# A two-layer transformer kernel, down products of layer 0's experts: a third chunk buffer, loads asked for three chunks ahead, and the gate product placed just ahead of its reader

## The chip, the core and the metric

The kernel runs on one core of a Trainium2 chip as one program of 66,430 instructions. The core has four engines that compute: TensorE (PE, with its weight loads shown as PEld), VectorE (DVE), ScalarE (ACT) and GpSimd (POOL). Sixteen DMA engines move data between HBM and SBUF; transfers are asked for from queues, here that of SyncE (SP) for nearly all loads, that of ScalarE for writes, and that of GpSimd for gathers. Each engine and each queue works through its own list in order and waits on semaphores for the others. The metric is the device time of one execution in microseconds, as the median over runs.

## The reference

Two blocks of two layers each work on 256 tokens (and, in the first block, on 256 context tokens) of width 1024, in float32. The part that matters here is the expert stage of layer 0 of the first block, `peer_ffn`: each token picks, in 8 heads, 16 of 16,384 experts, whose up rows give a hidden value and whose down rows are summed up with gate times hidden value.

```python
def chunk(xc):
    ...
    top_s, pos = lax.top_k(cand, PEER_TOPK)
    eidx = jnp.take_along_axis(cidx, pos, axis=-1)
    gate = jax.nn.softmax(top_s, axis=-1)
    u = u_emb[eidx]
    hid = jax.nn.gelu(jnp.einsum('td,thkd->thk', xc, u))
    wgt = (gate * hid.astype(jnp.float32)).astype(xc.dtype)
    return jnp.einsum('thk,thkd->td', wgt, v_emb[eidx])
```

## The kernel before

For 384 of the 512 tokens of layer 0 the kernel does not gather expert rows. It computes the hidden values of all 16,384 experts (the up products, 128 steps of 128 experts, `"u"`), multiplies them by a dense matrix that holds the gates and zeros elsewhere, and multiplies the result with all down rows (the down products, 128 steps, `"vv"`). The last 128 tokens are gathered instead: `gathered()` fetches one row a token with an indirect DMA on GpSimd's queue (line 1399, four tiles `gr` in turn) and VectorE works on each (line 1408 for up rows, line 1423 for down rows). `sp` in the code is true in layer 0 alone.

Every float32 matrix product runs as three products of halves: ScalarE copies the high half (`wh`, `Wh`), VectorE subtracts it for the low half (`wl`, `Wl`). For streamed weights, `Stream` does this: `_load` asks for a 512 KB tile `raw` on SP's queue (line 200, five buffers), `_high` (line 212) and `_low` (line 223) split it two steps ahead of its use. The order of all streamed tiles is one list; down tiles (`in_vv`) and tiles for the next layer's modulation (`in_modt`, used by VectorE at line 516) alternate in it.

The up products write their hidden values through the tiles `gstage` (two steps of experts and 384 KB each, line 1642) to HBM, `gel` (line 1647), and the gate matrix is built beside them and written as `gmat` (line 1536). The down products read both back in 32 chunks of four steps:

- `wload(c)` (lines 1593 to 1598) asks on SP's queue for `gelc` and `gmc`, 768 KB each, two buffers each.
- `wmul(c)` (line 1604 in layer 0) multiplies `gelc` by `gmc` in place, on VectorE.
- `wsplit(i)` (line 1616, recorded at lines 472 and 473) splits the 384 columns of step i into `Wh` and `Wl`, four buffers each. It runs two steps ahead of the matmuls.
- `vmm` (line 1692) does 18 matmuls a step: three token tiles, three products of halves, two halves of the 1024 columns.

In step i, with chunk c and r = i mod 4, the calls stand in this order:

```python
if r == 0 and c + 1 < nch:
    wmul(c + 1)
if i + 2 < 128:
    wsplit(i + 2)
if r == CI - 1 and c + 2 < nch:
    wload(c + 2)
hl = W.next("vv", l, i, 1 if i >= 126 else None)
```

`W.next` is where the loads and the splits of later down tiles are put into the queues. The steps of `gathered()` are put between them by a planner, `Side`, which holds a clock of assumed costs: `tick` advances it with each group of matmuls, `took` charges VectorE or ScalarE. So a call that stands elsewhere also moves some gather steps on VectorE by a place or two. The first two chunks are asked for in step 118 of the up products, and `wmul(0)` runs in its step 125.

Of the kernel before, what the change touches and what calls it, by code (L numbers as in the profile page):

```python
# [10 lines left out]
F32 = mybir.dt.float32  # L11
F32R = mybir.dt.float32r
# [47 lines left out]
def late_v(i):  # L60

    n = (i - 1) * 48 // 122
    return (n,) if 0 < i <= 122 and n < i * 48 // 122 else ()
# [341 lines left out]
def tile_dit_peer_conformer(ctx: ExitStack, tc: tile.TileContext, A, out):  # L405
# [7 lines left out]
    def bankA():  # L413
        return psum.tile([128, 512], F32, name="pA", bufs=4)
# [51 lines left out]
    def mm3(o, s, m, start, stop):  # L466
        nc.tensor.matmul(o, s[0], m[0], start=start, stop=False)  # L467
        nc.tensor.matmul(o, s[0], m[1], start=False, stop=False)  # L468
        nc.tensor.matmul(o, s[1], m[0], start=False, stop=stop)  # L469

    def split(h, lo, src):
        nc.scalar.activation(h, src, AF.Copy)  # L472
        nc.vector.tensor_sub(lo, src, h.bitcast(F32))  # L473
# [37 lines left out]
    def mod_tile(l, n, S, junk):  # L511

        raw = W.next("modt", l, n)
        for s in range(2 if l == 0 or n < 16 else 1):
            o = modc[l][:, n, s:s + 1]
            nc.vector.scalar_tensor_tensor(junk, raw, 1.0, S[:, s], op0=OP.mult, op1=OP.mult, accum_out=o)
            spend("v", 1300)
        made.add((l, n))
        n0 = n // 8 * 8
        if all((l, n0 + k) in made for k in range(8)):  # L520
            g = modc[l][:, n0:n0 + 8, :]
            nc.vector.tensor_add(g, g, pc(l, "bmod")[:, n0:n0 + 8, None].to_broadcast([128, 8, 2]))
# [7 lines left out]
    def gate_row(pool, l, m, s):  # L530
        t = pool.tile([128, D], F32, name="grow", bufs=2)
        for hf in range(2):
            p = bankB()
            for j in range(4):
                nc.tensor.transpose(p[:, j * 128:(j + 1) * 128],
                                    modc[l][:, m * 8 + hf * 4 + j, s:s + 1].to_broadcast([128, 128]), ident)
            nc.scalar.activation(t[:, hf * 512:(hf + 1) * 512], p, AF.Copy)
        return t
# [110 lines left out]
    def tick(dt):  # L649
        if cur["side"] is not None:  # L650
            cur["side"].tick(dt)
# [618 lines left out]
    def peer(l, hcp, kp, keys, early):  # L1270
        last = l == NL - 1
        sp = not last
# [3 lines left out]
        TD = T - 128 if sp else T  # L1276
        ntd = TD // 128
        TB = 32
        ntb = TD // TB
        CI = 2048 // T  # L1280
# [4 lines left out]
        with ExitStack() as st:  # L1285
# [7 lines left out]
            gp = st.enter_context(tc.tile_pool(name=f"gel{l}", bufs=3))  # L1293
# [29 lines left out]
            def took(eng, ns):  # L1323
                return cur["side"].spend(eng, ns) if sp and cur["side"] else 0.0
# [265 lines left out]
            nch = 128 // CI  # L1590
            ld, ww = {}, {}

            def wload(c):
                g = vq.tile([128, CI, TD], F32, name="gelc", bufs=2)
                nc.sync.dma_start(g, gel_d[c])
                m = vq.tile([128, ntb, CI, TB], F32, name="gmc", bufs=2)
                nc.sync.dma_start(m, g_d[:, :, c * CI:(c + 1) * CI, :].rearrange("b p c t -> p b c t"))
                ld[c] = (g, m)

            def wmul(c):  # L1600
                g, m = ld[c]
                if sp:
                    gv = g.rearrange("p c (b t) -> p c b t", t=TB)
                    nc.vector.tensor_mul(gv, gv, m.rearrange("p b c t -> p c b t"))
                    took("v", 1770)
                    return
                for ci in range(CI):
                    gv = g[:, ci].rearrange("p (b t) -> p b t", t=TB)
                    nc.gpsimd.tensor_mul(gv, gv, m[:, :, ci])  # L1609

            def wsplit(i):
                c, r = divmod(i, CI)
                g = ld[c][0]
                wh = vp.tile([128, TD], F32R, name="Wh", bufs=4)
                wl = vp.tile([128, TD], F32R, name="Wl", bufs=4)
                split(wh, wl, g[:, r])
                if sp:
                    took("a", 470)
                    took("v", 560)
                ww[i] = (wh, wl)  # L1620

            gs = None
            b = None
            GB = 2 if not last else 4
            per = 512 // T
            for i in range(128):
                if i == WS:
                    wsplit(0)
                    wsplit(1)
                if i % GB == 0:  # L1630
                    gs = gp.tile([128, GB, TD], F32, name="gstage", bufs=3)
                h, lo = W.next("u", l, i)
                half = i % per
                if half == 0:
                    b = bankA()
                o = b[:, half * TD:(half + 1) * TD]
                for d in range(8):
                    mm3(o, (h[:, d * 128:(d + 1) * 128], lo[:, d * 128:(d + 1) * 128]), (X[0][:, d, :TD], X[1][:, d, :TD]), d == 0, d == 7)
                    tick(3 * TD / 2.4)
                if half == per - 1:  # L1640
                    j = i % GB - (per - 1)
                    nc.scalar.activation(gs[:, j:j + per].rearrange("p a t -> p (a t)"), b[:, :per * TD], AF.Gelu_apprx_tanh)
                    if sp:
                        took("a", 500)
                if i % GB == GB - 1:
                    c, r = divmod(i - GB + 1, CI)
                    nc.scalar.dma_start(gel_d[c][:, r:r + GB], gs)
                    if sp:
                        took("a", 340)
                if l == 0 and i in LATE:  # L1650
                    mod_tile(0, 40 + LATE.index(i), S, junk)
                if i == 118:
                    if sp:
                        side.finish(sel)
                    else:
                        side.drain()
                        cur["side"] = W.side = None
                    tk_stack.close()
                    vp = st.enter_context(tc.tile_pool(name=f"pv{l}", bufs=2))
                    vq_stack = ExitStack()  # L1660
                    vq = vq_stack.enter_context(tc.tile_pool(name=f"pw{l}", bufs=2))
                    wload(0)
                    wload(1)
                    if l == 0:
                        def turn():
                            for _ in angles(vq):
                                yield (side.spend("p", 2500.0) + 4000.0, None, 0, 0.0, 0.0, 0.0)
                        side.add(turn())
                        side.lanes.reverse()
                if i == 122:  # L1670
                    rows = [gate_row(vp, l, 5, s) for s in range(ns)]
                if i == 125:
                    wmul(0)
# [14 lines left out]
            def vmm(t, i, w, hl, halves=(0, 1)):  # L1688
                sh, sl = (x[:, t * 128:(t + 1) * 128] for x in w)
                for n, (s_, m_) in enumerate(((sh, hl[0]), (sh, hl[1]), (sl, hl[0]))):  # L1690
                    for dh in halves:
                        nc.tensor.matmul(acc[t][dh], s_, m_[:, dh * 512:(dh + 1) * 512],  # L1692
                                         start=(i == 0 and n == 0), stop=(i == 127 and n == 2))
                if sp:
                    tick(3 * len(halves) * 512 / 2.4)

            for i in range(128):
                c, r = divmod(i, CI)
                if r == 0 and c + 1 < nch:
                    wmul(c + 1)  # L1700
                if i + 2 < 128:
                    wsplit(i + 2)
                if r == CI - 1 and c + 2 < nch:
                    wload(c + 2)
                hl = W.next("vv", l, i, 1 if i >= 126 else None)
                if i >= 126:
                    held.append((i, ww.pop(i), hl))
                    continue
                w = ww.pop(i)
                for t in range(ntd):  # L1710
                    vmm(t, i, w, hl)
                for n in late_v(i) if sp else ():
                    mod_tile(l + 1, n, S, junk)
# [555 lines left out]
    with tc.tile_pool(name="hcp", bufs=1) as hcp:  # L2269
        tail = peer(0, hcp, kp, *first)  # L2270
        kp = ExitStack()
        first = mixer(1, kp, tail, done=xp)
    peer(1, None, kp, *first)
    with tc.tile_pool(name="b2", bufs=1) as b2p:
        dec = b2p.tile([128, RET_H, 384], F32, name="dec")
# [161 lines left out]
```

## Time and profile before

| | |
|---|---|
| median of 3 runs | 4544.48 us (4543.31 to 4550.07) |
| profiled execution, its own time | 4539.79 us |
| its span, first to last instruction | 4538.0 us |
| mean granted TensorE clock | 0.96 of full |
| PE / PEld busy | 4215.3 us (93%) / 3735.4 us (82%) |
| DVE busy | 3221.3 us (71%) |
| ACT busy | 1970.2 us (43%) |
| POOL busy | 1128.6 us (25%) |
| DMA | 932.29 MB, mean 205 GB/s |

The shares are means over stages with different limits. The down products of layer 0 lie between 1441 and 2213 us of the span. Engine names in the views are those given above; L1604 is line 1604 of the kernel; a group of instructions is named by its output and inputs, as `gelc<-gelc,gmc`; "idle before" is the time that the engine stood still just ahead of them, with the instruction or transfer that ended it. A DMA share is the busy share of the 16 DMA engines; packets of several queues can overlap, so it can pass 1.

### The profile page before, as it was taken

Reading aid. Unit: us, or ns where it says so; the run is one execution under the profiler, and the core shown is the slowest. Engines: PE = TensorE matmul, PEld = TensorE weight load, DVE = VectorE, ACT = ScalarE, POOL = GpSimd, SP = SyncE. Lnnn points to the kernel's source line nnn. Section 1 sums busy time; section 2 is a strip of 40 time slices with the busy share of each in tenths; the row PEclk is TensorE's granted clock in tenths of the full one; section 3 lists DMA queues with packets and bytes.
Section 4 is the critical chain, followed back from the end, with each engine's and each line's share of the span. In section 5 each row is a group of like instructions: output and inputs, shape, how many; then the busy total and the mean of one; then the engine's idle time right before and its main releaser. Section 6 shows DMA issues by size and latency. Waiting matters only on the chain. (4 is left out here: it accounts for less than half of the span.)

```text
span 4538.0 us, 66430 instructions
## 1 busy us (share of the span) xinstructions
PE 4215.3 (93%) x25423; PEld 3735.4 (82%) x25423; DVE 3221.3 (71%) x5177; ACT 1970.2 (43%) x2939; POOL 1128.6 (25%) x871
## 2 busy tenths in 40 slices
PE   8999999999998877777779989999999999999999
PEld 5887878999997666666678879999887998999988
DVE  6747766999996766566786878786666577555855
ACT  4224443334662222222334444575445445444544
POOL 0012343333117412222543446201443000000000
PEclk9999999999999888888899989999999999999999
DMA  6532232456889877878783336778886644556344
GB/s 218 166 99 69 72 101 97 151 194 234 293 293 343 278 259 270 289 276 283 249 301 110 107 124 206 237 282 306 281 280 237 215 154 132 187 181 215 116 160 156
DMA packets 304824, 932.29 MB, mean 205 GB/s; under 512 B 27752, under 2 KB 95736, under 8 KB 299640
## 3 DMA queue, kind: packets, MB, share of 16 engines
q1 hardware_dynamic: 244000, 696.86, 46.1%
q0 software_dynamic: 37040, 135.29, 8.3%
q10 hardware_dynamic: 23464, 95.88, 5.6%
q8 instruction: 199, 3.26, 0.3%
q14 instruction: 121, 0.99, 0.1%
HBM read 841.94 MB, written 85.99 MB: 204 GB/s over the span
## 5 line engine op out<-in xcount | busy, mean ns | idle before, releaser
L212 ACT ACTIVATE wh<-raw 128x1024 fp32r<-128x1024 f32 (+1 forms) x1086 | 1131.4, 1045 | 1093.4 <-DMA raw<-in_vv 516.4
L469 PE MATMUL pA<-xH,wl 128*128 128x256 f32 (+2 forms) x4600 | 1422.0, 309 | 57.3 <-DVE wl L223 46.1
L223 DVE TENSOR_TENSOR wl<-raw,wh 128x1024 fp32r<-128x1024 f32 (+2 forms) x956 | 1185.5, 1249 | 365.2 <-issue 185.5
L467 PE MATMUL pA<-xH,wh 128*128 128x256 f32 (+2 forms) x4600 | 1439.6, 313 | 1.7 <-ACT xH L472 1.3
L468 PE MATMUL pA<-xL,wh 128*128 128x256 f32 (+2 forms) x4600 | 1417.2, 308 | 0.5 <-DVE xL L473 0.3
L469 PEld LDWEIGHTS pA<-xH,wl 128*128 128x128 f32 x4600 | 876.1, 190 | 93.0 <-DVE wl L223 55.4
L467 PEld LDWEIGHTS pA<-xH,wh 128*128 128x128 f32 x4600 | 877.0, 191 | 34.8 <-issue 6.0
L468 PEld LDWEIGHTS pA<-xL,wh 128*128 128x128 f32 x4600 | 877.1, 191 | 26.6 <-DVE xL L473 1.1
L223 POOL TENSOR_TENSOR wl<-raw,wh 128x1024 fp32r<-128x1024 f32 (+1 forms) x130 | 322.8, 2484 | 731.8 <-PE pA L469 362.8
L1692 PE MATMUL pA<-wl,Wh 128*128 128x512 f32 x1024 | 349.9, 424 | 150.4 <-DVE wl L223 150.4
L1692 PEld LDWEIGHTS pA<-wl,Wh 128*128 128x128 f32 x1024 | 203.2, 202 | 211.1 <-DVE wl L223 163.9
L1692 PE MATMUL pA<-wh,Wl 128*128 128x512 f32 x1024 | 344.5, 419 | 1.7 <-DVE Wl L473 1.7
L1692 PE MATMUL pA<-wh,Wh 128*128 128x512 f32 x1024 | 335.3, 409 | 6.2 <-ACT Wh L472 6.2
L1399 POOL DMA_INDIRECT gr<-in_ur,gi x128 | 185.8, 1451 | 530.9 <-DVE gr L1408 498.8
L468 PE MATMUL pA<-wl,xH 128*128 128x256 f32 (+2 forms) x800 | 272.1, 340 | 10.2 <-POOL wl L223 6.2
L467 PE MATMUL pA<-wh,xH 128*128 128x256 f32 (+2 forms) x800 | 277.9, 347 | 1.8 <-ACT xH L472 1.8
L469 PE MATMUL pA<-wh,xL 128*128 128x256 f32 (+2 forms) x800 | 271.5, 339 | 1.1 <-DVE xL L473 1.1
L1399 POOL DMA_INDIRECT gr<-in_vr,gi x128 | 176.3, 1377 | 340.1 <-DVE gx L1423 297.7
L1609 POOL TENSOR_TENSOR gelc<-gelc,gmc 128x256 f32<-128x256 f32 x128 | 147.9, 1189 | 422.4 <-DMA gmc<-gmat 398.6
L1692 PEld LDWEIGHTS pA<-wh,Wl 128*128 128x128 f32 x1024 | 206.8, 202 | 54.5 <-DVE Wl L473 2.4
L1692 PEld LDWEIGHTS pA<-wh,Wh 128*128 128x128 f32 x1024 | 200.3, 196 | 56.2 <-ACT Wh L472 6.5
L458 POOL TENSOR_TENSOR segr<-segr,nhalf 128x1 f32<-128x1 f32 (+1 forms) x24 | 13.9, 579 | 886.3 <-DVE segr L547 886.3
(456 smaller groups left out, 6305.4 us busy)
## 6 DMA issues: line engine op xcount, KB each, us to landing
raw<-in_u SPq DMA_DIRECT2D x256, 512.0 KB
raw<-in_vv SPq DMA_DIRECT2D x256, 512.0 KB
raw<-in_modt SPq DMA_DIRECT2D x80, 512.0 KB
gmat<-gst ACTq DMA_DIRECT2D x20, 2048.0 KB
raw<-in_conv SPq DMA_DIRECT2D x48, 512.0 KB
raw<-in_gate SPq DMA_DIRECT2D x48, 512.0 KB
gel<-gstage ACTq DMA_DIRECT2D x64, 384.0 KB
gelc<-gel SPq DMA_DIRECT2D x32, 768.0 KB
```

What stands on the lines that cost most here:

```text
L212: self.nc.scalar.activation(h[:, :w], t[:, :w], AF.Copy)
L223: e.tensor_sub(lo[:, :w], t[:, :w], h[:, :w].bitcast(F32))
L458: nc.gpsimd.tensor_tensor(r, r, nhalf[:, 0:1].to_broadcast([128, w]), op=OP.pow)
L467: nc.tensor.matmul(o, s[0], m[0], start=start, stop=False)
L468: nc.tensor.matmul(o, s[0], m[1], start=False, stop=False)
L469: nc.tensor.matmul(o, s[1], m[0], start=False, stop=stop)
L1399: nc.gpsimd.indirect_dma_start(t, None, tabs[j // 128], bass.IndirectOffsetOnAxis(ap=gi[:, k:k + 1], axis=0))
L1609: nc.gpsimd.tensor_mul(gv, gv, m[:, :, ci])
L1692: nc.tensor.matmul(acc[t][dh], s_, m_[:, dh * 512:(dh + 1) * 512], start=(i == 0 and n == 0), stop=(i == 127 and n == 2))
```

## The change

In layer 0 alone, `gelc` and `gmc` get three buffers instead of two, three chunks are asked for ahead of the stage instead of two, and in the stage chunk c + 3 is asked for in step r = 2 of chunk c instead of chunk c + 2 in step r = 3. The product of chunk c + 1 moves from step r = 0 to step r = 2, where its first split stands. To make room in SBUF, `Wh` and `Wl` go from four buffers to three each and `gstage` from three to two.

```diff
@@ -1591,9 +1591,9 @@
             ld, ww = {}, {}
 
             def wload(c):
-                g = vq.tile([128, CI, TD], F32, name="gelc", bufs=2)
+                g = vq.tile([128, CI, TD], F32, name="gelc", bufs=3 if sp else 2)
                 nc.sync.dma_start(g, gel_d[c])
-                m = vq.tile([128, ntb, CI, TB], F32, name="gmc", bufs=2)
+                m = vq.tile([128, ntb, CI, TB], F32, name="gmc", bufs=3 if sp else 2)
                 nc.sync.dma_start(m, g_d[:, :, c * CI:(c + 1) * CI, :].rearrange("b p c t -> p b c t"))
                 ld[c] = (g, m)
 
@@ -1611,8 +1611,8 @@
             def wsplit(i):
                 c, r = divmod(i, CI)
                 g = ld[c][0]
-                wh = vp.tile([128, TD], F32R, name="Wh", bufs=4)
-                wl = vp.tile([128, TD], F32R, name="Wl", bufs=4)
+                wh = vp.tile([128, TD], F32R, name="Wh", bufs=3 if sp else 4)
+                wl = vp.tile([128, TD], F32R, name="Wl", bufs=3 if sp else 4)
                 split(wh, wl, g[:, r])
                 if sp:
                     took("a", 470)
@@ -1628,7 +1628,7 @@
                     wsplit(0)
                     wsplit(1)
                 if i % GB == 0:
-                    gs = gp.tile([128, GB, TD], F32, name="gstage", bufs=3)
+                    gs = gp.tile([128, GB, TD], F32, name="gstage", bufs=2 if sp else 3)
                 h, lo = W.next("u", l, i)
                 half = i % per
                 if half == 0:
@@ -1659,8 +1659,8 @@
                     vp = st.enter_context(tc.tile_pool(name=f"pv{l}", bufs=2))
                     vq_stack = ExitStack()
                     vq = vq_stack.enter_context(tc.tile_pool(name=f"pw{l}", bufs=2))
-                    wload(0)
-                    wload(1)
+                    for c in range(3 if sp else 2):
+                        wload(c)
                     if l == 0:
                         def turn():
                             for _ in angles(vq):
@@ -1696,11 +1696,13 @@
 
             for i in range(128):
                 c, r = divmod(i, CI)
-                if r == 0 and c + 1 < nch:
+                if r == (CI - 2 if sp else 0) and c + 1 < nch:
                     wmul(c + 1)
                 if i + 2 < 128:
                     wsplit(i + 2)
-                if r == CI - 1 and c + 2 < nch:
+                if sp and r == CI - 2 and c + 3 < nch:
+                    wload(c + 3)
+                if not sp and r == CI - 1 and c + 2 < nch:
                     wload(c + 2)
                 hl = W.next("vv", l, i, 1 if i >= 126 else None)
                 if i >= 126:
```

On VectorE, near the middle of the stage. Before (`gelc_14582` is chunk 12, `gelc_14447` chunk 11; `wl` are splits of down tiles, `gr` gather steps, `sjunk` modulation steps):

```order
L1604 TENSOR_TENSOR gelc_14582<-gelc_14582,gmc_14584 128x1536
L473 TENSOR_TENSOR Wl_14617<-gelc_14447,Wh_14616 128x384
L223 TENSOR_TENSOR wl_14622<-raw_14522,wh_14586 128x1024
L1408 SCALAR_TENSOR_TENSOR gr_14470,gz_5918<-gr_14470,gx_5917 128x1024
L516 SCALAR_TENSOR_TENSOR sjunk_5907,modc1_98<-raw_14488,S_5906 128x1024
L473 TENSOR_TENSOR Wl_14649<-gelc_14447,Wh_14648 128x384
L223 TENSOR_TENSOR wl_14656<-raw_14558,wh_14620 128x1024
L1408 SCALAR_TENSOR_TENSOR gr_14479,gz_5918<-gr_14479,gx_5917 128x1024
L473 TENSOR_TENSOR Wl_14682<-gelc_14582,Wh_14681 128x384
```

The product stands two splits ahead of the last two readers of the chunk before; its own first reader is the last row. After (`gelc_14423` is chunk 12, `gelc_14292` chunk 11):

```order
L1408 SCALAR_TENSOR_TENSOR gr_14483,gz_5918<-gr_14483,gx_5917 128x1024
L516 SCALAR_TENSOR_TENSOR sjunk_5907,modc1_98<-raw_14491,S_5906 128x1024
L473 TENSOR_TENSOR Wl_14655<-gelc_14292,Wh_14654 128x384
L223 TENSOR_TENSOR wl_14662<-raw_14569,wh_14621 128x1024
L1408 SCALAR_TENSOR_TENSOR gr_14540,gz_5918<-gr_14540,gx_5917 128x1024
L1604 TENSOR_TENSOR gelc_14423<-gelc_14423,gmc_14425 128x1536
L473 TENSOR_TENSOR Wl_14689<-gelc_14423,Wh_14688 128x384
L223 TENSOR_TENSOR wl_14698<-raw_14597,wh_14660 128x1024
```

The product now stands directly ahead of its first reader, behind the last split of the chunk before.

On the load queue (SP), the same place. Before (`gel0_12` and `gel0_13` are the chunks, `raw` the streamed tiles):

```order
L1595 DMA gelc_14582<-gel0_12_5870 128x1536
L1597 DMA gmc_14584<-gmat0_5890 128x12x128
L200 DMA raw_14590<-in_vv 128x1024
L200 DMA raw_14624<-in_vv 128x1024
L200 DMA raw_14652<-in_modt 128x1024
L200 DMA raw_14658<-in_vv 128x1024
L200 DMA raw_14689<-in_vv 128x1024
L1595 DMA gelc_14717<-gel0_13_5871 128x1536
L1597 DMA gmc_14719<-gmat0_5890 128x12x128
```

The pair of chunk 13 stands one step ahead of its product. After:

```order
L1595 DMA gelc_14559<-gel0_13_5871 128x1536
L1597 DMA gmc_14561<-gmat0_5890 128x12x128
L200 DMA raw_14563<-in_modt 128x1024
L200 DMA raw_14569<-in_vv 128x1024
L200 DMA raw_14597<-in_vv 128x1024
L200 DMA raw_14625<-in_vv 128x1024
L200 DMA raw_14658<-in_modt 128x1024
L200 DMA raw_14664<-in_vv 128x1024
L1595 DMA gelc_14692<-gel0_14_5872 128x1536
L1597 DMA gmc_14694<-gmat0_5890 128x12x128
```

The pairs stand in the same rhythm between the streamed tiles, but each belongs to a chunk that is multiplied eight steps later.

## Rows read from the trace of the kernel before

**Rows 1.** Groups by line, 1496.5 to 2173.8 us: busy, mean ns | idle before, releaser
```profile
L1692 PE MATMUL pA<-wl,Wh 128*128 128x512 f32 x452 | 166.9, 454 | 137.4 <-DVE wl L223 137.4
...
L212 ACT ACTIVATE wh<-raw 128x1024 fp32r<-128x1024 f32 x112 | 118.7, 1060 | 505.2 <-DMA raw<-in_vv 484.3 <-PE pB L1692 20.9
...
L1604 DVE TENSOR_TENSOR gelc<-gelc,gmc 128x1536 f32<-128x1536 f32 x29 | 51.0, 1758 | 243.9 <-DMA gmc<-gmat 243.9
```

**Rows 2.** Timeline of VectorE through one chunk: start, duration, instruction
```profile
1720.93 0.08 DVE L1408 DVE_READ_ACCUMULATOR gr<-gr,gx 128x1 f32 x1
1730.02 1.76 DVE L1604 TENSOR_TENSOR gelc<-gelc,gmc 128x1536 f32<-128x1536 f32 x1 [9.00 <-DMA gmc<-gmat]
```

**Rows 3.** Timeline of the load queue (SP) in the same stretch
```profile
1716.42 0.43 SPq L1595 DMA_DIRECT2D gelc<-gel  x1
1716.89 0.44 SPq L1597 DMA_DIRECT2D gmc<-gmat  x1
...
1722.68 13.85 SPq L200 DMA_DIRECT2D raw<-in_vv  x3
```

**Rows 4.** Windows of 2 us: PE, PEld, DVE, ACT, POOL busy, granted clock, DMA share, GB/s
```profile
1728.00:1730.00 2.00, 0.87 (x4) 0.38 (x2) 0.00 (x0) 0.00 (x0) 0.00 (x0) 1.00 1.05 397
1730.00:1732.00 2.00, 0.00 (x0) 0.00 (x0) 1.98 (x2) 0.00 (x0) 0.00 (x0) 0.95 0.24 94
1732.00:1734.00 2.00, 0.56 (x1) 0.50 (x2) 2.00 (x3) 1.47 (x2) 0.00 (x0) 0.50 0.00 0
```

**Rows 5.** Timeline of VectorE: first and last of the 29 waiting products
```profile
1496.56 1.76 DVE L1604 TENSOR_TENSOR gelc<-gelc,gmc 128x1536 f32<-128x1536 f32 x1 [1.98 <-DMA gmc<-gmat]
...
2173.78 1.76 DVE L1604 TENSOR_TENSOR gelc<-gelc,gmc 128x1536 f32<-128x1536 f32 x1 [10.03 <-DMA gmc<-gmat]
```

**Rows 6.** Timeline of TensorE behind a wait: pairs of matmuls
```profile
1709.39 1.22 PE L1692 MATMUL pA<-wl,Wh 128*128 128x512 f32 x2 [3.57 <-DVE wl L223]
...
1711.26 1.05 PE L1692 MATMUL pA<-wh,Wh 128*128 128x512 f32 x2
1712.11 1.05 PE L1692 MATMUL pA<-wl,Wh 128*128 128x512 f32 x2
...
1713.82 1.05 PE L1692 MATMUL pB<-wh,Wh 128*128 128x512 f32 x2
...
1716.58 0.63 PE L1692 MATMUL pA<-wh,Wl 128*128 128x512 f32 x2
1717.05 0.63 PE L1692 MATMUL pA<-wh,Wh 128*128 128x512 f32 x2
```

**Rows 7.** Windows: 70 us ahead of the stage, and the 28 chunks
```profile
1360.00:1430.00 70.00, 59.30 (x321) 57.07 (x321) 41.71 (x60) 23.06 (x33) 44.66 (x51) 0.95 1.01 377
1496.50:2173.80 677.30, 538.53 (x2038) 421.60 (x2036) 432.20 (x536) 167.94 (x229) 173.75 (x130) 0.87 0.80 276
```

**Rows 8.** DMA view of the 28 chunks: packets and bytes
```profile
DMA packets 86737, 187.23 MB, mean 276 GB/s; under 512 B 5255, under 2 KB 48263, under 8 KB 86705
```

**Rows 9.** Groups by line, the 28 chunks: the split of W on ScalarE
```profile
L472 ACT ACTIVATE Wh<-gelc 128x384 fp32r<-128x384 f32 x112 | 56.9, 508 | 0.0
```

**Rows 10.** Timeline of ScalarE and its queue in the up products
```profile
1136.67 0.33 ACTq L1536 DMA_DIRECT2D gmat<-gst  x1
...
1138.58 0.33 ACTq L1647 DMA_DIRECT2D gel<-gstage  x1
...
1153.13 0.54 ACT L1642 ACTIVATE gstage<-pA 128x384 f32<-128x384 f32 x1
```

**Rows 11.** The page's DMA issues: the write of the gate matrix
```profile
gmat<-gst ACTq DMA_DIRECT2D x20, 2048.0 KB
```

**Rows 12.** Waits from 1450 to 1480 us: total, times, longest
```profile
DVE gr L1408 <- DMA gr<-in_ur,gi: 10.4, 5, 5.0
```

**Rows 13.** Window of 50 us at the start of the stage, columns as in rows 4
```profile
1450.00:1500.00 50.00, 41.73 (x169) 32.80 (x169) 37.51 (x49) 11.78 (x16) 44.15 (x51) 0.91 0.89 311
```

**Rows 14.** Groups by line, the 28 chunks: gather steps of the second table
```profile
L1423 DVE SCALAR_TENSOR_TENSOR gx<-gr,gz,gx 128x1024 f32<-128x1024 f32 x62 | 79.4, 1280 | 1.9 <-DMA gr<-in_vr,gi 1.2
```

## The prediction

> **What bounds the kernel now.** I read the costliest groups by line over the down stage of layer 0 first. Three rows tell the story [rows 1]: VectorE waited 243.9 us, in 29 products at line 1604, for `gmc`; TensorE stood still 137.4 us for the split weights that VectorE makes behind that product; ScalarE, 505.2 us idle against 118.7 us of weight splits, is no limit. Second, the timeline of VectorE through one chunk [rows 2]: it has finished everything else at 1721.01, and its next instruction, the product, begins at 1730.02; only behind that, in its order, come the `Wl` and `wl` that TensorE waits for. Third, the timeline of the load queue [rows 3]: the two loads that this product waits for were asked for at 1716.42 and 1716.89, 13.1 us before it could begin, and in program order one step of the loop ahead of it. Fourth, 2 us windows around the wait [rows 4]: the DMA engines are full (1.05) while VectorE waits, then fall to 0.24 and to 0.00. That fall is the loss: while VectorE is held, no raw buffer comes free, so nothing new is asked for, and once the late chunk has landed the engines have nothing to move. TensorE pays twice, first idle and then, behind the idle time, at half clock (granted 0.50 at 1732, so 1.2 GHz where 2.4 is full).
>
> How long is a chunk? The first and the last of the 29 waiting products begin at 1496.56 and 2173.78 [rows 5], 28 chunks apart: 677.2 / 28 = 24.19 us.
>
> **What a chunk would take if nothing were late**, from three resources over the same 677 us.
> - TensorE: 4 steps of 18 matmuls. At full clock two follow each other in 0.47 us (1716.58 to 1717.05), at half clock in 0.85 (1711.26 to 1712.11) [rows 6]. 36 pairs by 0.467 is 16.8 us.
> - VectorE: 432.2 us busy over 28 chunks [rows 7], 15.4 us. Nothing on it is added or taken away; the order changes.
> - DMA: share 0.80 of 24.19 us [rows 7] is 19.35 us of packets, 187.23 MB in all [rows 8], 6.69 MB a chunk. Full engines are seen just ahead of the stage, 1360 to 1430: share 1.01 at 377 GB/s [rows 7]. By the share a chunk then takes 19.35 / 1.01 = 19.2 us, by the rate 6.69 / 0.377 = 17.7 us.
>
> So DMA is the longest of the three, at 17.7 to 19.2 us, and a wait of 8.4 us (243.9 / 29) can't be won in full: some 5 us of it can.
>
> **The change part by part.**
> *Load three ahead, third buffer.* Chunk c+3 is asked for in step 4c+2, and multiplied in step 4c+10: eight steps, at 16.8 / 4 us each 33.6 us, against the 13.1 us that a load took with full engines [rows 3]. The buffer that it needs was last read by the splits of step 4c+1, so the load queue finds it free and no load behind it waits longer. The 29 waits on `gmc` go. What is late next is the weight tile itself: ScalarE already waits for `in_vv` through most of the stage [rows 1], and with DMA full that wait reaches TensorE through the same split. So I put a chunk at 19.2 us, the end given by the share, because a chain with few buffers between its engines hardly runs at its best rate. 28 x (24.19 - 19.2) = 139.7 us saved. A half-clock stretch for each chunk fits inside: from 1709.39 to the pair at 1713.82 there are 6 pairs [rows 6], each 0.85 us where 0.467 would do, 2.3 us in all, and 16.8 + 2.3 = 19.1.
>
> *Product ahead of its reader.* Before, two steps of splits stood between product and first reader; now `Wl` follows it at once, and the `Wh` between them runs on ScalarE. VectorE stands for one `Wh`, 0.51 us by its mean [rows 9], each chunk: 15.4 + 0.5 = 15.9 us, still under 19.2. Cost nothing, cover DMA; without that cover 28 x 0.5 = 14 us.
>
> *Wh and Wl three buffers instead of four.* The split of step i+2 now needs TensorE done with step i-1. The `wl` of the same step has three buffers already and waits for the same end, so no chain grows by more than the 0.51 us of `Wh` ahead of it, with two steps of matmuls, 8.4 us, in between. Nothing.
>
> *gstage two buffers instead of three.* In the up products a gelu now needs the write of two pairs back landed. A write asked for at 1138.58, behind a 2048 KB `gmat` write from 1136.67, has until the gelu at 1153.13: 14.6 us [rows 10, 11]. Both writes, 2.49 MB, take 6.6 us at 377 GB/s, 13.2 at half of that. Nothing, and little if late, for four PSUM banks lie between gelu and TensorE.
>
> *Third chunk loaded ahead of the stage.* Two more loads stand on the load queue ahead of the last `in_u` tiles, in the stretch where DMA is full [rows 7]: 1.57 MB / 377 GB/s = 4.2 us later. The bytes are missing later, at the first load inside the stage, so the cost is between 0 and 4.2 us; I take 2.1.
>
> **The sum.** -139.7 + 2.1 = -137.6 us. Against the profiled execution, 4539.79 us, that is 4402.2; against the median of the three runs, 4.7 us higher, 4544.48 - 137.6 = **4407 us**.
>
> **Rivals.**
> *Engines that compute set the pace (0.15).* DMA delivers more than its share suggests. For it: 2 us windows in the stage reach 397 GB/s [rows 4], and by rate a chunk needs 17.7 us: 28 x 6.49 = 182 us, with the start 4365. At TensorE's own 16.8 us, 28 x 7.39 = 207 us, 4340. Against it: over 70 us the full engines gave 377 and no more [rows 7]. The Trainium skill (HBM Reference, Specifications (TRN2)) says that a core streaming alone measures about 425 GB/s, as this core is; by that 6.69 MB take an estimated 15.7 us, and DMA would bound nothing. The trace does not bear it out with this mix of tiles: its longest full stretch is 11% lower.
>
> *Gathers come late (0.19).* With DMA full, the rows that POOL gathers may become the wait that replaces `gmc`, on the same engine and with the same `wl` behind it. For it: from 1450 to 1480, about one chunk, VectorE waited 10.4 us for them, five times [rows 12]. Against it: POOL was then busy 44.15 of 50 us [rows 13] with other work between its gathers, and over the later 28 chunks VectorE waited 1.9 us for the second table [rows 14]. Each gather is asked for four gathers ahead. VectorE becomes the bound when such waits pass 19.2 - 15.9 = 3.3 us a chunk. At half of the 10.4 us, 5.2, a chunk takes 21.1 us: 28 x 3.1 = 87 us saved, with the 2.1 above 4460. The Trainium skill (DMA: Bandwidth & Descriptors, Queues, rings and completion order) says that each DMA engine takes turns between the queues that have work, a packet at a time; by that a longer load queue halves a gather's rate at worst and does not hold it back, which is why this case is not the likeliest. No row here separates the two queues inside a window.
>
> *Slower (0.06).* The same mechanism in full, at its place behind each product: from 24.19 - 15.9 = 8.3 us of gather waits a chunk the kernel loses. At 10.4 us a chunk takes 26.3: 28 x 2.1 = 59 us, with the start 4606. It needs POOL or the gather queue to be as late in all 28 chunks as in that one.
>
> *The wait stays (0.05).* The load queue is held by full raw buffers so long that the chunk's load still goes out just ahead of its product. Then 4544. Against it: the order gives eight steps, and even the 13.85 us that the queue took over three raw tiles from 1722.68 [rows 3] would leave 19.7 of 33.6.
>
> **How the numbers follow.** The forecast, 18.5 to 20.2 us a chunk (4387 to 4435 with the start), gets 0.55; the rivals have 0.15, 0.19, 0.06 and 0.05. The range reaches from 4360, just beyond the rate's end of 17.7 us, to 4462, the half-sized gather wait; it leaves out the part of the first rival below 17.7 us, the heavier gather waits, and the last two cases, some 0.2. Faster by over 0.2%, about what a measurement of this kernel can tell from no change (9 us), holds for the forecast and the first two rivals: 0.55 + 0.15 + 0.19 = 0.89. Within 0.2%: 0.05. Slower: 0.06.
>
> **What would show it.** In the profile of the changed kernel: the row of line 1604 with almost no wait on `gmc`; 28 chunks in some 538 us instead of 677, by the beginnings of its products; DMA share over the stage near 1 without windows of 0.0; ScalarE's wait for `in_vv` as the longest, and TensorE's idle time before line 1692 well under 137 us. Gather waits of more than 3 us a chunk on line 1408 or 1423 would show the second rival; a DMA share well under 1 with VectorE busy throughout, the first. The step most likely wrong is the choice of 19.2 us: every microsecond of it is 28 in the sum.

## The result, and the profile after

The changed kernel takes 4356.01 us (median of 4 runs, 4355.36 to 4360.71) against 4543.9 us (median of 4, 4533.0 to 4550.07): ratio 0.9591, 95% interval 0.9572 to 0.9611. That is 188 us less where 137.6 were forecast; the time lies 4 us under the range. The direction and the place were right, the size was not.

The profiled execution took 4355.36 us, its span 4353.6, so 184.4 us less than before. First the groups by line over the stretch that answers to [rows 1, 9, 14], here 1498.3 to 1998.2 us, for the same 28 chunks: busy, mean ns of one | idle before, releaser.

```profile
L1692 PE MATMUL pA<-wl,Wh 128*128 128x512 f32 x446 | 143.9, 404 | 12.5 <-DVE wl L223 12.4
...
L212 ACT ACTIVATE wh<-raw 128x1024 fp32r<-128x1024 f32 x112 | 118.0, 1053 | 215.9 <-DMA raw<-in_vv 190.7 <-PE pB L1692 21.5 <-DVE Wl L473 1.9
...
L1423 DVE SCALAR_TENSOR_TENSOR gx<-gr,gz,gx 128x1024 f32<-128x1024 f32 x65 | 83.2, 1280 | 0.8
...
L473 DVE TENSOR_TENSOR Wl<-gelc,Wh 128x384 fp32r<-128x384 f32 x112 | 62.3, 556 | 63.6 <-ACT Wh L472 60.3 <-PE pB L1692 1.5 <-ACT wh L212 1.1
L472 ACT ACTIVATE Wh<-gelc 128x384 fp32r<-128x384 f32 x112 | 57.4, 512 | 115.3 <-DVE gelc L1604 97.5 <-PE pB L1692 17.6
L1408 DVE SCALAR_TENSOR_TENSOR gr<-gr,gx 128x1024 f32<-128x1024 f32 x48 | 57.2, 1219 | 0.0
L1604 DVE TENSOR_TENSOR gelc<-gelc,gmc 128x1536 f32<-128x1536 f32 x29 | 50.9, 1754 | 0.0
```

The wait of line 1604 is gone entirely, 243.9 to 0.0 us; TensorE's wait for `wl` fell from 137.4 to 12.4; ScalarE still waits for `in_vv`, 190.7 us, as the longest. The gathers, lines 1408 and 1423, wait 0.0 and 0.8 us. On VectorE one wait is new: `Wl` for `Wh`, 60.3 us.

Second, the first and the last of the same 29 products, which answer to [rows 5].

```profile
1498.38 1.80 DVE L1604 TENSOR_TENSOR gelc<-gelc,gmc 128x1536 f32<-128x1536 f32 x1
...
1998.11 1.75 DVE L1604 TENSOR_TENSOR gelc<-gelc,gmc 128x1536 f32<-128x1536 f32 x1
```

The 28 chunks take 499.73 us, 17.85 each, where they took 677.2 and 24.19. So 177.5 of the 184.4 us lie in them. The stage from its first to its last matmul went from 767.7 us (1444.1 to 2211.8) to 586.3 (1443.3 to 2029.6), 181.4 less: 3.9 us more come from its first and last chunks, and 3.0 from all that lies outside.

Third, the windows that answer to [rows 7] and to the 2 us windows of [rows 4]: PE, PEld, DVE, ACT, POOL busy, granted clock, DMA share, GB/s.

```profile
1498.30:1998.20 499.90, 480.50 (x2010) 378.44 (x2009) 434.84 (x536) 166.25 (x229) 190.51 (x134) 0.99 1.01 370
...
1700.00:1980.00 280.00, 269.26 (x1139) 211.78 (x1138) 245.20 (x280) 92.50 (x127) 112.97 (x72) 1.00 1.03 386
...
1728.00:1730.00 2.00, 2.00 (x10) 1.63 (x9) 2.00 (x4) 0.28 (x1) 0.44 (x1) 1.00 1.08 424
1730.00:1732.00 2.00, 2.00 (x10) 1.59 (x10) 1.97 (x6) 0.00 (x0) 1.70 (x2) 1.00 0.99 380
1732.00:1734.00 2.00, 2.00 (x10) 1.60 (x9) 1.46 (x1) 0.37 (x1) 0.48 (x1) 1.00 1.01 395
1734.00:1736.00 2.00, 1.17 (x6) 0.62 (x4) 1.81 (x3) 2.00 (x4) 0.00 (x0) 1.00 1.08 364
```

DMA is full nearly throughout (of 249 windows of 2 us 8 lie under 0.8, the lowest at 0.46), and the windows of 0.24 and 0.00 are gone. With them went nearly all half-clock stretches: the granted clock over the chunks rose from 0.87 to 0.99 of 2.4 GHz. The third view, DMA of 1500 to 2000 us, answers to [rows 8].

```profile
DMA packets 84896, 185.13 MB, mean 370 GB/s; under 512 B 5207, under 2 KB 46679, under 8 KB 84865
...
q1 hardware_dynamic: 68388, 124.75, 69.0%
q0 software_dynamic: 16477, 59.99, 31.6%
```

At the mean rate of the 28 chunks, 370 GB/s over 499.9 us, a chunk moved 6.61 MB. That a chunk takes as long as its bytes need at this rate follows from how the rate is worked out; whether the rate is what sets the chunk, the experiments have to show.

Last, VectorE and the load queue in the middle of the stage, as in [rows 2, 3].

```profile
1731.71 1.75 DVE L1604 TENSOR_TENSOR gelc<-gelc,gmc 128x1536 f32<-128x1536 f32 x1
1734.19 0.56 DVE L473 TENSOR_TENSOR Wl<-gelc,Wh 128x384 fp32r<-128x384 f32 x1 [0.73 <-PE pB L1692]
...
1746.79 0.56 DVE L473 TENSOR_TENSOR Wl<-gelc,Wh 128x384 fp32r<-128x384 f32 x1 [3.11 <-ACT Wh L472]
...
1749.38 1.75 DVE L1604 TENSOR_TENSOR gelc<-gelc,gmc 128x1536 f32<-128x1536 f32 x1
```
```profile
1694.04 0.38 SPq L1595 DMA_DIRECT2D gelc<-gel  x1
...
1711.22 0.39 SPq L1595 DMA_DIRECT2D gelc<-gel  x1
...
1728.60 0.42 SPq L1595 DMA_DIRECT2D gelc<-gel  x1
...
1748.97 0.63 SPq L1595 DMA_DIRECT2D gelc<-gel  x1
```

Chunk loads go out every 17 to 20 us, two products ahead of their own, and the products start without a wait.

### The profile page after: what moved, and what is told of

Read it like the earlier page. It is cut to its first block, busy times and chain, and to the rows that moved or that the text cites. A ratio compares the mean times of both kernels' runs of the same rounds, so it can differ in the third digit from the quotient of the medians.

```text
span 4353.6 us, 66325 instructions
## 1 busy us (share of the span) xinstructions
PE 4159.8 (96%) x25423; PEld 3695.3 (85%) x25423; DVE 3226.9 (74%) x5177; ACT 1968.1 (45%) x2939; POOL 1139.9 (26%) x871
## 5 line engine op out<-in xcount | busy, mean ns | idle before, releaser
L1692 PE MATMUL pA<-wl,Wh 128*128 128x512 f32 x1024 | 326.9, 400 | 15.9 <-DVE wl L223 15.8
L1692 PE MATMUL pA<-wh,Wh 128*128 128x512 f32 x1024 | 325.7, 399 | 7.6 <-ACT Wh L472 7.6
L1692 PE MATMUL pA<-wh,Wl 128*128 128x512 f32 x1024 | 325.0, 398 | 2.7 <-DVE Wl L473 2.7
L1692 PEld LDWEIGHTS pA<-wl,Wh 128*128 128x128 f32 x1024 | 191.9, 189 | 70.1 <-DVE wl L223 24.6
L1399 POOL DMA_INDIRECT gr<-in_vr,gi x128 | 191.9, 1500 | 222.7 <-DVE gx L1423 188.4
L473 DVE TENSOR_TENSOR Wl<-gelc,Wh 128x384 fp32r<-128x384 f32 (+1 forms) x256 | 138.8, 543 | 137.3 <-ACT Wh L472 133.3
```

Source lines behind the costliest of these rows:

```text
L1399: nc.gpsimd.indirect_dma_start(t, None, tabs[j // 128], bass.IndirectOffsetOnAxis(ap=gi[:, k:k + 1], axis=0))
```

## The experiments

The theory: in the stage DMA is now the bound, at its full rate in bytes. Rivals: TensorE is the bound; the product's new place costs or gives something of its own; and the small buffers cost something. The second question is which part of the change gave the time.

### e1, the product back in its old place

```diff
-                if r == (CI - 2 if sp else 0) and c + 1 < nch:
+                if r == 0 and c + 1 < nch:
                     wmul(c + 1)
```

> The changed kernel with the product of chunk c+1 put back to step r=0; three buffers and loads three ahead stay. Its chunk takes 17.85 us and the kernel 4356 us. Theory A, the DMA engines set the chunk (6.61 MB at 370 GB/s is 17.9 us): the loads stand where they stood, so 4356 within 6 us. Theory B, VectorE sets it, because it stands for Wh behind each product (60.3 us of Wl waiting for Wh between 1500 and 2000): the wait goes and the kernel is faster by 20 us or more, 4336 or less. In both, no wait on gmc comes back, since six steps lie between load and product.

Measured: 4354.21 us (4350.15 to 4357.83), ratio 0.9595 (0.9579 to 0.9611), the changed kernel's own within its interval. With the longer lead alone all of the time is gained. The new wait is not the product's doing either: `Wl` waits 58.8 us for `Wh` here too (1500 to 1980 us).

```profile
L473 DVE TENSOR_TENSOR Wl<-gelc,Wh 128x384 fp32r<-128x384 f32 x107 | 59.7, 557 | 58.8 <-ACT Wh L472 58.8
```

### e2, the product's place alone

The kernel before, with two buffers and its old load place.

```diff
-                if r == 0 and c + 1 < nch:
+                if r == (CI - 2 if sp else 0) and c + 1 < nch:
                     wmul(c + 1)
```

> The kernel before with only the product moved to step r=2, ahead of its reader; two buffers, loads two ahead in step r=3, Wh, Wl and gstage as before. The load then has three steps, some 12.6 us, until its product instead of one, and it took 13.1 us in the trace of before. Theory L, the lead is what counted and the third buffer only adds to it: nearly all of the gain, a chunk of 18 to 19 us, 4360 to 4400. Theory M, a load asked for so late still comes behind queued tiles and the wait shrinks only by the two steps won, half of it or more stays: 4430 to 4500.

Measured: 4360.67 us (4349.7 to 4367.49), ratio 0.9601 (0.9578 to 0.9624). So either half of the change gives nearly all of it by itself, and the third buffer is not needed. A load asked for in step 3 of one chunk and read in step 2 of the next has three steps. Line 1604 keeps a rest of its wait (1500 to 1980 us):

```profile
L1604 DVE TENSOR_TENSOR gelc<-gelc,gmc 128x1536 f32<-128x1536 f32 x27 | 47.4, 1755 | 5.6 <-DMA gmc<-gmat 5.6
```

### e3, two matmuls in eighteen left out

```diff
                 for n, (s_, m_) in enumerate(((sh, hl[0]), (sh, hl[1]), (sl, hl[0]))):
+                    if sp and t == 2 and n == 1:
+                        continue
```

> The changed kernel with 16 of the 18 matmuls of a step of the down products of layer 0: the product of the high half of the hidden values with the low half of the down rows is left out for the third token tile. Everything else stands in the same order. Theory A, DMA sets the chunk: 4356 within 8 us. Theory C, TensorE sets it (it is busy 96% of the stage): 8 matmuls fewer a chunk at 0.233 us are 1.9 us, 32 chunks 60 us, 4296 to 4310.

Measured: 4351.7 us (4349.1 to 4355.39), ratio 0.9589 (0.9573 to 0.9605). A ninth less to do for TensorE buys nothing: the engine stands still longer, 480 - 433 us against 480 - 463 in the same window of the changed kernel, and DMA moves as much as ever. TensorE was not the bound. First the window of the changed kernel, then that of e3:

```profile
1500.00:1980.00 480.00, 462.70 (x1943) 364.78 (x1942) 415.74 (x516) 160.49 (x221) 179.19 (x128) 0.99 1.01 372
```
```profile
1500.00:1980.00 480.00, 433.31 (x1719) 333.11 (x1717) 416.80 (x514) 158.74 (x219) 178.91 (x123) 0.95 1.01 373
```

### e4, one more transfer a chunk

```diff
                     wload(c + 3)
+                    nc.sync.dma_start(dram.tile([128, 1024], F32, name=f"spare{c}"), A["vv"][l, c])
```

> The changed kernel with one more transfer a chunk behind the chunk's loads on the same queue: 512 KB of down rows copied within HBM to a place that nobody reads, 29 times. Theory A, DMA sets the chunk: 0.52 MB at 370 GB/s is 1.4 us a chunk, 41 us in all, 4397 (4385 to 4410). Theory C, TensorE sets it and DMA has room: 4356 to 4366.

Measured: 4388.57 us (4381.28 to 4390.75), ratio 0.9663 (0.9645 to 0.9681); against the changed kernel's 0.9591 that is 0.0072 of 4540, 33 us. The sign and the order of size are those of DMA as the bound: 15.2 MB of copies that no engine waits for lengthen the stage, whose last matmul moves from 2029.6 to 2064.9 us. 15.2 MB in these 35 us is 431 GB/s, more than the stage's mean, so the added tiles were cheaper than the mix that they joined, or a part of them found idle engines; which of the two was not separated. The window of 1500 to 1980 us shows the rate unchanged, the same bytes and fewer matmuls than the changed kernel's 1943.

```profile
1500.00:1980.00 480.00, 444.17 (x1807) 344.70 (x1806) 386.52 (x483) 148.23 (x205) 162.02 (x113) 0.97 0.99 371
```

### e5, without the loads of the modulation tiles

```diff
-        if i in self.pre:
+        if i in self.pre or self.order[i][:2] == ("modt", 1):
             return True
...
         raw = W.next("modt", l, n)
+        if l == 1:
+            raw = S[:, 0]
```

> The changed kernel without the 48 loads of layer 1's modulation weights in the down products; VectorE works on a tile that lies in SBUF already, with as many instructions as before. Theory A, DMA sets the chunk at 370 GB/s: 25.2 MB less are worth 68 us until another engine sets the pace; TensorE's 16.8 us a chunk stop it at 17.97 - 16.8 = 1.2 us in 31 chunks, 36 us: 4320 to 4335. Theory B, VectorE sets it (86% busy and 60 us of waits for Wh): no gain, 4350 to 4360.

Measured: 4322.72 us (4317.96 to 4332.58), ratio 0.952 (0.9491 to 0.9549), in the range expected of DMA as the bound. Layer 1's modulation is not computed here; the run shows time alone. VectorE, with as many instructions as before, did not hold it back. With 48 tiles fewer to load TensorE becomes the bound, busy in 479 of 480 us, and its own pace shows: its wait for `wl` is 0.8 us, and the 32 products stand 16.93 us apart on average (1438.5 to 1963.2 us), against the 16.8 worked out from [rows 6].

```profile
1500.00:1980.00 480.00, 479.19 (x2055) 384.56 (x2053) 446.68 (x548) 171.07 (x233) 197.06 (x134) 1.00 0.97 343
```

The edit takes away bytes and, with them, the raw buffers that the tiles held; e4, which adds bytes and takes no buffer, points the same way. A DMA share near 1 does not by itself show the bound: it is 0.97 here too, beside 343 GB/s.

### e6, both at once

e5 with the two matmuls of e3 left out as well.

> The run without the modulation loads, and with 16 of 18 matmuls a step as in the run with fewer matmuls (one product of halves left out for the third token tile). If TensorE is what stops that run, TensorE now needs 14.9 us a chunk and DMA 5.8 MB / 370 GB/s = 15.7: faster than it by 20 to 35 us. If VectorE stops it (15.4 us of work and its waits), no faster than it by more than 8 us.

Measured: 4310.89 us (4306.51 to 4315.02), ratio 0.9495 (0.9469 to 0.952): 11.8 us less than e5, and no run of either lies in the range of the other. The same edit that bought nothing in e3 buys something here, so TensorE did bound e5. It buys less than the 20 us and more than the 8 that the two cases expected: TensorE now waits 16.4 us for `wl` and 10.3 for `Wh` (1500 to 1980 us), so it is no longer alone the bound. VectorE is busy 451 of the 480 us and DMA at a share of 0.97; which of them sets the pace now was not separated.

```profile
L1696 PE MATMUL pA<-wl,Wh 128*128 128x512 f32 x460 | 151.0, 409 | 16.6 <-DVE wl L223 16.4
...
L1696 PE MATMUL pA<-wh,Wh 128*128 128x512 f32 x460 | 148.0, 402 | 10.3 <-ACT Wh L472 10.3
```

### e7, the small buffers alone

The kernel before with the changed kernel's three `Wh`, three `Wl` and two `gstage`.

```diff
-                wh = vp.tile([128, TD], F32R, name="Wh", bufs=4)
-                wl = vp.tile([128, TD], F32R, name="Wl", bufs=4)
+                wh = vp.tile([128, TD], F32R, name="Wh", bufs=3 if sp else 4)
+                wl = vp.tile([128, TD], F32R, name="Wl", bufs=3 if sp else 4)
...
-                    gs = gp.tile([128, GB, TD], F32, name="gstage", bufs=3)
+                    gs = gp.tile([128, GB, TD], F32, name="gstage", bufs=2 if sp else 3)
```

> The kernel before with only the room given up: Wh and Wl in three buffers, gstage in two; loads and product where they were. My prediction costed both at nothing: 4544 within 9 us. The rival: the tighter reuse of Wh or the write of gstage costs 0.5 us a step of the down products or of the up products, 64 us: 4590 or more.

Measured: 4541.18 us (10 runs, 4528.78 to 4548.41), ratio 0.9994 (0.9981 to 1.0006). The buffers given up cost nothing under the old wait. As they cost less than 0.1% there, and e2, which keeps the larger buffers, is no faster than the changed kernel, no price of theirs shows after the change either.

### e8, sixteen modulation tiles moved out of the stage

If bytes are the bound, bytes moved to a stretch that has room should pay. Tiles 32 to 47 go to the gate products of layer 1.

```diff
-    n = (i - 1) * 48 // 122
-    return (n,) if 0 < i <= 122 and n < i * 48 // 122 else ()
+    n = (i - 1) * 32 // 122
+    return (n,) if 0 < i <= 122 and n < i * 32 // 122 else ()
...
                     order.extend(("modt", 0, m) for m in gate_slots(k, b))
+                else:
+                    order.append(("modt", 1, 32 + 2 * k + b))
...
```

> The changed kernel with 16 of the 48 modulation tiles of layer 1 (32 to 47) taken out of the down products and worked on in layer 1's gate products, where DMA was busy 0.39 and VectorE 52% (2200 to 2250). All work is done. Theory A: 8.4 MB less in the stage at 370 GB/s are 22.7 us; the gate products take 16 steps of VectorE more, 18 us beside TensorE's work: 4333 to 4345. Rival: the gate products pay it back, because each such tile holds a raw buffer there and VectorE's split comes late: 4350 to 4365.

Measured: 4350.48 us (4347.11 to 4357.99), ratio 0.9576 (0.9551 to 0.9602), which the changed kernel's interval overlaps. The bytes did not leave the stage. The planner puts gather steps where VectorE is free, and it filled the freed time with 143 of them between the first product and the last, 126 before the edit. Between 1500 and 1980 us second-table gathers went from 60 to 77 steps, and the rate stayed at 373 GB/s.

```profile
L1437 DVE SCALAR_TENSOR_TENSOR gx<-gr,gz,gx 128x1024 f32<-128x1024 f32 x77 | 98.6, 1281 | 13.0 <-DMA gr<-in_vr,gi 12.2
```

### e9, the same with the planner still charged

e8, with the planner's clock charged for the steps that have left, so that it plans as many gathers as before. `here` gives nothing for every third of the 48 places, so that 32 tiles stay in the stage.

```diff
...
                 for n in late_v(i) if sp else ():
-                    mod_tile(l + 1, n, S, junk)
+                    if here(n) is None:
+                        took("v", 1300)
+                    else:
+                        mod_tile(l + 1, here(n), S, junk)
```

> As the run with 16 modulation tiles moved to layer 1's gate products, but the planner is still charged for the moved tiles in the down products, so that it puts as many gather steps there as in the changed kernel (126 between the first and the last product; 143 in that run). All work is done. Theory A, bytes set the stage: now 8.4 MB really leave it, 22.7 us at 370 GB/s, with TensorE at 16.8 us a chunk close behind: 4333 to 4345. Rival: what leaves the stage is paid back in the gate products, through VectorE's tiles or the raw buffers: 4350 to 4360.

Measured: 4361.65 us (5 runs, 4356.32 to 4370.7), ratio 0.9622 (0.9598 to 0.9646): no gain. In the stage the bytes did what bytes should: its last matmul comes at 2006.5 us instead of 2029.6, 23.1 us earlier, where 22.7 had been worked out. The rest of the kernel then took 2347.9 us instead of 2324.0, so all of it was given back. The place shows in the second 100 us behind the stage, first of the changed kernel, then of e9, whose moved steps run from 2128.8 to 2212.3 us.

```profile
2129.60:2229.60 100.00, 86.96 (x636) 83.37 (x635) 74.54 (x90) 38.07 (x55) 36.17 (x30) 0.93 0.72 255
```
```profile
2106.50:2206.50 100.00, 72.19 (x482) 68.04 (x481) 84.03 (x111) 30.30 (x45) 29.60 (x28) 0.86 0.82 300
```

TensorE does 15 us less work there. The waits of ScalarE's weight copies in these two stretches, in the same order, say what came late:

```profile
L212 ACT ACTIVATE wh<-raw 128x1024 fp32r<-128x1024 f32 x25 | 25.8, 1052 | 18.0 <-PE pA L469 8.2 <-PE pA L468 7.7 <-issue 1.8
```
```profile
L219 ACT ACTIVATE wh<-raw 128x1024 fp32r<-128x1024 f32 x18 | 18.9, 1056 | 54.9 <-DMA raw<-in_gate 25.8 <-DMA raw<-in_co 20.6 <-DMA raw<-in_v 4.4
```

The weight tiles of the gate products are now waited for, 46.4 us, where the changed kernel waits 0.4. DMA is not full there (0.82), so the moved tiles most likely stand in the way of the others, on the load queue or in its buffers; which of the two, and how much VectorE, busy 84 us in 100, adds by freeing buffers late, was not separated.

### e10, the product one step later

The kernel before, with the product in step 1 of the chunk: two steps behind its load instead of one.

```diff
-                if r == 0 and c + 1 < nch:
+                if r == (1 if sp else 0) and c + 1 < nch:
                     wmul(c + 1)
```

> The kernel before with the product moved by one step only, to r=1; two buffers, loads two ahead in step r=3. The lead from load to product is two steps, one more than before and one less than in the run with the product alone moved (4361 us). Theory L, the wait is the landing time less the lead: one step of 4.2 us off 8.4 leaves about half the wait, and the gain is somewhat over half, 4420 to 4460. Rival: any lead beyond one step lets the transfers run on, because VectorE frees raw buffers in the step won: most of the gain at once, 4360 to 4400.

Measured: 4381.23 us (4375.17 to 4396.38), ratio 0.9653 (0.9627 to 0.968). The expectation of the theory, 4420 to 4460, missed, and the rival's range held: the wait is not a fixed landing time less the lead. The profiled execution is the slowest of the four, 4396.38 us. In it the wait of a waiting product fell from 8.41 us (243.9 / 29) to 2.78 (69.5 / 25 over the stage), 5.6 us for one step. Measured from the ask for `gmc` on the load queue, the waiting products before began after 13.35 us on average (29), VectorE having come to them after 4.94; here after 11.34 us (25), VectorE having come after 8.56. So 3.6 of the 5.6 us are lead, and 2.0 are that the chunk landed sooner. Why it did was not tried, nor was the rival's reason, that raw buffers come free in the step won; fewer transfers starting again behind a stop would do it too. Between 1500 and 1980 us:

```profile
L1604 DVE TENSOR_TENSOR gelc<-gelc,gmc 128x1536 f32<-128x1536 f32 x25 | 43.9, 1758 | 67.3 <-DMA gmc<-gmat 67.3
```

So by steps between load and product, the waits of all 32 products and the time: one, 243.9 us and 4544; two, 69.5 and 4381 (ratio 0.9653); three (e2), 6.1 and 4361 (0.9601); six (e1) and eight (the change), none, 4354 and 4356 (0.9595 and 0.9591).

## Why the prediction was off

**The step that failed is the choice of 19.2 us for a chunk.** It stood between the end given by the share, 19.2, and the end given by the rate, 17.7, and took the former "because a chain with few buffers between its engines hardly runs at its best rate". Measured: 17.85. That is 28 x 1.35 = 37.8 us of the miss. With the same five raw buffers the chain did run at nearly the best rate: 370 GB/s over 500 us, against the 377 of [rows 7] over 70. The 2.3 us of half clock that were to fit inside 19.2 were not needed either, with a granted clock of 0.99. That the rate's end came so near to 17.85 is in part luck: 377 is 1.9% above the 370 that the stage gave, and 6.69 MB a chunk 1.2% above the 6.61 that its window held, and the two errors work against each other.

**Why the share misled.** It took the 0.80 share of the 28 chunks for work that stays the same, 19.35 us of packets a chunk. But in the kernel before, bytes took longer at some times than at others. Two windows of it, one just behind a wait, where transfers start again, and one with the engines full (the first holds weight tiles alone, the second chunk and gathered rows):

```profile
1736.00:1738.00 2.00, 2.00 (x6) 1.52 (x6) 2.00 (x4) 1.08 (x2) 1.72 (x1) 0.50 0.45 139
...
1748.00:1750.00 2.00, 2.00 (x10) 1.60 (x9) 0.00 (x0) 1.25 (x2) 0.00 (x0) 1.00 0.99 405
```

139 GB/s at a share of 0.45 is 309 for a full share, 405 at 0.99 is 409. Over all 28 chunks it was 276 / 0.80 = 345 before and 370 / 1.01 = 366 after. A chunk's packets took 0.80 x 24.19 = 19.35 us before and 1.01 x 17.85 = 18.0 after; some 0.2 us of the difference are the 1.2% of bytes. Packets of one size on one queue show it without the mix: a 4096-byte packet of the load queue took 159 ns in the median before and 160 after, but 188 and 170 in the mean, and 9.4% and 3.3% of them passed 220 ns. They are slowest where loads start again: those that began 4 to 5 us behind the start of a product took 345 ns in the mean (698 packets in 27 chunks). The part of the share that went with the stops was no work of the chunk, and it went away with them. What makes them slow behind a stop was not tried, and stays open.

**The rest of the miss**, 50 us in all (187.9 against 137.6), is 12.5 us. The start, put at +2.1, cost nothing that shows: the first matmul of the stage comes 0.8 us earlier, and the first and last chunks of the stage gave 3.9 us. Another 3.0 lie outside the stage, and 3.5 between the profiled executions and the medians. 2.1 + 3.9 + 3.0 + 3.5 = 12.5.

**Right as argued.** The waits on `gmc` went, all 29. What became late next is the weight tile by way of ScalarE, its longest wait, and reaches TensorE as 12.4 us. DMA is the longest resource, as e3, e4 and e5 show, at 17.85 us, with TensorE close behind at its predicted 16.8 (16.93 in e5). Buffers given up cost nothing (e7). The product ahead of its reader cost nothing, but its cover was needed more than the 0.51 us a chunk foresaw: `Wl` waits 2.2 us a chunk for `Wh` (60.3 / 28). ScalarE does `Wh` in its own order, behind `wh` copies that wait for `in_vv`; with the loads relieved in e5 the wait halves, to 29.1 us. It is not the price of the product's new place, as e1 has it in full with the product in the old one; that it costs time no run shows, and none separates it.

**The rivals.** That DMA delivers more than its share suggests is what happened, at its 17.7 us end and not at TensorE's pace. The sign given for that rival, a DMA share well under 1, did not come: the share was 1.01, and the chunk shorter all the same. The Trainium skill (HBM Reference, Specifications (TRN2)) gives about 425 GB/s for a core that streams alone; that was reached here only in single windows of 2 us (431 from 1504 and from 1556 us), while 280 us gave 386 and 500 us gave 370, with tiles in long runs, `gelc` and `gmc` chunks and gathered rows mixed. A chunk estimated by that page would have been 15.7 us, under TensorE's pace, and e3 shows that TensorE was not the pace. The gathers were not late: 0.8 us of waits in 28 chunks with both queues at work, 69.0% and 31.6% of the engines. The Trainium skill (DMA: Bandwidth & Descriptors, Queues, rings and completion order) has each engine take turns between the queues with work, which agrees: a full load queue did not hold gathers back. The waits of [rows 12] stayed what they were, something of the stage's start: 6.8 us at line 1408 between 1443 and 1500. The load that stays late, and the slower kernel, did not come.

## What to carry to other kernels

When a wait goes and DMA becomes the bound, size the new pace by bytes over the rate that full engines show, not by the busy share times the old time: a share that was measured with stops in it holds packet time that goes with the stops. On an engine that works in order, a product placed one step behind its load stops everything behind it, the buffers that feed the load queue too; a step or two more of lead takes nearly all of that, by an earlier load or by a later reader, and a third buffer is only one of the ways. Where bytes are the bound, moving them pays only if the stretch that takes them has room on the load queue, in its buffers and on the engines as well, and a planner that fills freed time can put other bytes in their place.

## What was not expected of the hardware

The time that DMA engines spend on the same bytes is not constant: 309 GB/s for a full share in a window behind a stop, 409 in a full one, 345 and 366 over the whole stage before and after, and 345 ns in place of 160 for a packet of 4096 bytes where loads start again. And the sustained rate was the same in every kernel that filled the engines, whatever was changed beside it: 367 to 373 GB/s between 1500 and 1980 us in e1, e2, e3, e4, e8, e9 and the changed kernel, with the product in either place and two or three chunk buffers.
